# Three kept pieces instead of two in a down projection, with a new order table, in a two-layer attention encoder

## The chip, the cores and the metric

The kernel runs on one core of a Trainium2 chip. The metric is the device time of one execution in microseconds. A core has five instruction queues that run side by side: PE (matrix products and transposes), ACT (functions and copies), DVE (elementwise work), POOL (elementwise work and some transfers) and SP (transfers). Results of PE land in eight banks of 128 x 512 fp32 numbers, from which ACT and DVE read.

## The reference

Two layers over 512 tokens of width 1024, in fp32. Layer 0 mixes tokens with neighbourhood attention on a grid of 8 x 64, layer 1 with three groups of dilated attention. Each mixer ends in an output projection, and each layer in a SwiGLU block of inner width 2816:

```python
def swiglu(x, w_gate, w_up, w_down):
    return (jax.nn.silu(x @ w_gate) * (x @ w_up)) @ w_down
...
    for layer in range(DEPTH):
        h = rms_norm(x, norm_mix_pre[layer])
...
            h = neighbourhood_attention(h, na_w_qkv[j], na_w_o[j], na_rpb[j])
...
            h = dilated_attention(h, dil_w_qkv[j], dil_w_o[j])
        x = x + rms_norm(h, norm_mix_post[layer])
        h = rms_norm(x, norm_ffn_pre[layer])
        x = x + rms_norm(swiglu(h, ffn_w_gate[layer], ffn_w_up[layer], ffn_w_down[layer]), norm_ffn_post[layer])
```

## The kernel before

**Products.** Every fp32 operand is split into a high part h (ACT's copy, L415) and a low part l (DVE's subtraction, L416), and each fp32 product is three products of such parts (`mm3`, L426 to L430, so that one product shows as L427, L428 and L429). L427 and L429 read the high part of the moving operand, L428 its low part. Over blocks of the matrices runs a scheme with seven products in place of eight (`Seven`); its sums of weights are made on POOL and DVE (L495 to L501).

**Stages.** The time runs through: layer 0's projections and attention (to about 210 us), its output projection (tile names yo), gate and up projection (gu), down projection (yd); then the same for layer 1, whose attention runs from 590 to 1105 us. Tokens come in four tiles of 128. Between the output projection and the gate and up projection each tile is normed and transposed on PE (tr_o0_t_i: layer 0, tile t, part i; L649). A transpose's bank is emptied by ACT (L651, high part) and DVE (L652, low part); there are two such banks. L686 and L687 square and scale a half of a finished row of tiles, L633 and L635 (POOL) make its reciprocal root, L693 adds it to x.

**Down projection** (`down`, L937 to L1063). The inner width is cut into six pieces, five of two slots and one of one. For each piece the activations and the weights are split (`operands2`; the split weights take one of four slots), then multiplied into two banks, one for each of two tiles of tokens (`prod`, with ms the tiles done). The last two of the seven products both add into `left`, of which `left[0]` is tile 2 and `left[1]` tile 3. There the last pieces are kept and done for one tile, then for the other:

```python
                if i > last - 2:
                    kept.append(ops)
                else:
                    prod(left, ops)
...
        for m in range(2):
            for ops in kept:
                prod(left, ops, False, (m,))
```

**Order.** The order in which each queue runs its instructions isn't that of the code. `Order` collects all instructions with what they depend on, and `run` walks through them with costs of its own (`_cost`), taking on each engine the ready instruction of lowest rank. On PE it stays with the kind of the last matmul (plain, transposes, fp32) unless another is due by more than `stay`. `pin` (L317) repeats this forwards and backwards `times` times, takes the ranks of pass `FIRST`, and then goes through `TABLE`. A row of the table is (what, engine, lo, hi, turn, by): instructions of that engine (5: all) whose planned start (what 0 or 1) or whose number (what 2) lies from lo to hi get their rank moved by `by`, with what 0 from the rank they had in pass `turn`. One more walk gives the order, and each queue is tied to it.

Of the kernel before, what the change touches and what calls it, by code (L numbers as in the profile page):

```python
# [77 lines left out]
def _cost(i, e):  # L78
# [52 lines left out]

FIRST, TABLE = 11, (
# [28 lines left out]
)  # L163


class Order:
# [87 lines left out]
            for m in before:  # L254
                self.succ[m].append(n)

    stay = 1000.0

    def run(self, rank, back):

# [80 lines left out]
def encoder_kernel(ctx: ExitStack, tc: tile.TileContext, a: dict, out: bass.AP):  # L341
# [595 lines left out]
    def down(layer, hm, hl_, yp, more, sink):  # L937
# [3 lines left out]
        last = len(pieces) - 1  # L941
# [12 lines left out]
        def loaded(w):  # L954
            for i in range(last + 1):
                v = next(raw_)[:, :wp(w, i).shape[1]]
                nc.sync.dma_start(v, wp(w, i))
                yield v
# [75 lines left out]
        for n in range(2):  # L1034

            kept = []
            for i, w in enumerate(loaded(uab if n == 0 else every)):
                ops = operands2(xp((x1a, x2b)[n], i), w, f"{nm}{('s3', 'x2b')[n]}_{i}")
                if i > last - 2:
                    kept.append(ops)  # L1040
                else:
                    prod(left, ops)
                for f, *t in steps.get((n, i), ()):
                    f(*t)
            if n == 0:
# [3 lines that stand above are left out]
                    act.activation(y2u[m], left[m], AF.Copy)  # L1049
                for m in range(2):  # L1050
                    dve.tensor_sub(y2u[m], p5[m], y2u[m])
# [364 lines left out]
    order = [3 * j + g for j in range(PAIRS) for g in orders[j]]  # L1416
# [80 lines left out]
              for n, lo, hi, o, c, side in arenas]  # L1497
    order = Order(tc.nc.cur_bb.bb.instructions)
    order.link(tags, places, extra)
    order.pin(tc, 20, FIRST, TABLE)  # L1500


def _blocks(w, cols):
# [79 lines left out]
```

## Time and profile before

| | us |
|---|---|
| median of 3 runs | 1450.02 |
| lowest and highest run | 1445.73 and 1452.67 |
| the profiled execution | 1446.53 |
| its span, first to last instruction | 1444.7 |
| granted clock of PE, mean share of full speed | 0.997 |

The profile gives for each engine its busy time; for groups of instructions their line, their tile (out<-in) and form, busy time and mean; for a wait who waited and what ended it; and on a timeline each instruction with its start, its length and, in brackets, how long the engine stood idle before it and for whom. [...]

### The profile page before, as it was taken

How to read it: one execution, taken by the hardware profiler on the slowest of the kernel's cores; microseconds unless marked ns; L12 is line 12 of the kernel's file. 1: busy time of each engine (PE TensorE's matmuls, PEld its weight loads, DVE VectorE, ACT ScalarE, POOL GpSimd, SP SyncE). 2: the span in 40 equal slices, each digit the busy share in tenths (PEclk: the TensorE clock that was granted, in tenths of full speed). 3: DMA queues.
4: the chain of work that ended last, by engine and by line, in shares of the span. 5: the costliest groups of instructions: out<-in, count | busy, mean ns of one | idle time of the engine just before them, and what ended most of it. 6: DMA issues, size and time to landing. Idle time of an engine off the chain costs nothing. (4 is left out here: it accounts for less than half of the span.)

```text
span 1444.7 us, 27886 instructions
## 1 busy us (share of the span) xinstructions
PE 1412.8 (98%) x10764; PEld 1315.0 (91%) x10764; DVE 1182.1 (82%) x1882; ACT 905.0 (63%) x1822; POOL 557.4 (39%) x402
## 2 busy tenths in 40 slices
PE   7999999999999999999999999999999999999997
PEld 6988877999999888999989999999878999999886
DVE  6699967889998888888578777887657889998877
ACT  5478874555555657544477777887775555555664
POOL 5755525544330002766554434343215644340001
PEclk9999999999999999999999999999999999999999
DMA  6357587697234674445333343243766798844662
GB/s 235 112 181 193 168 298 211 217 268 205 89 117 147 196 229 158 162 159 183 125 103 111 111 146 120 82 139 104 253 185 245 200 246 236 261 142 154 209 213 95
DMA packets 86644, 253.20 MB, mean 175 GB/s; under 512 B 19312, under 2 KB 31600, under 8 KB 84464
## 3 DMA queue, kind: packets, MB, share of 16 engines
q1 hardware_dynamic: 77696, 197.69, 41.5%
q0 software_dynamic: 8672, 53.48, 14.4%
q8 instruction: 84, 1.38, 0.4%
q14 instruction: 48, 0.39, 0.1%
q10 hardware_dynamic: 144, 0.26, 0.0%
HBM read 229.24 MB, written 68.29 MB: 206 GB/s over the span
## 5 line engine op out<-in xcount | busy, mean ns | idle before, releaser
L635 POOL TENSOR_TENSOR rs_yd<-v_yd,mhalf 128x1 f32<-128x1 f32 x8 | 13.5, 1686 | 254.1 <-DVE v_yd L633 254.1
L427 PE MATMUL gu<-rxc,h_a 128*128 128x256 f32 x352 | 98.9, 283 | 1.4 <-ACT h_a L415 1.1
L428 PE MATMUL gu<-rxc,h_a 128*128 128x256 f32 x352 | 98.8, 281 | 1.3 <-DVE rxc L652 1.3
L429 PE MATMUL gu<-rxc,l_a 128*128 128x256 f32 x352 | 98.9, 282 | 0.0
L427 PE MATMUL gu<-rxa,h_c 128*128 128x256 f32 x352 | 98.5, 280 | 0.1
L429 PE MATMUL gu<-rxa,l_b 128*128 128x256 f32 x352 | 97.8, 278 | 0.2 <-DVE l_b L416 0.2
L428 PE MATMUL gu<-rxa,h_b 128*128 128x256 f32 x352 | 97.9, 278 | 0.2 <-DVE rxa L652 0.2
L428 PE MATMUL gu<-rxa,h_c 128*128 128x256 f32 x352 | 97.8, 278 | 0.0
L427 PE MATMUL gu<-rxa,h_b 128*128 128x256 f32 x352 | 97.8, 278 | 0.0
L429 PE MATMUL gu<-rxa,l_c 128*128 128x256 f32 x352 | 97.4, 278 | 0.0
L415 ACT ACTIVATE rxc<-mem 128x512 fp32r<-128x512 f32 (+2 forms) x92 | 57.6, 632 | 63.5 <-PE yd_pp L428 29.4
L495 POOL TENSOR_TENSOR r_d<-r_d 128x512 f32<-128x512 f32 x24 | 37.7, 1572 | 152.0 <-DVE l_ad L416 120.6
L416 DVE TENSOR_TENSOR rxc<-mem,rxc 128x512 fp32r<-128x512 f32 (+2 forms) x92 | 70.7, 776 | 20.6 <-ACT rxc L415 17.4
L495 POOL TENSOR_TENSOR r_gu<-r_gu 128x512 f32<-128x512 f32 x20 | 31.6, 1580 | 126.7 <-DVE l_a L416 69.8
L495 POOL TENSOR_TENSOR raw<-raw 128x512 f32<-128x512 f32 x24 | 40.3, 1682 | 91.6 <-DVE l_a L416 70.3
L427 PEld LDWEIGHTS gu<-rxc,h_a 128*128 128x128 f32 x352 | 67.0, 191 | 2.1 <-ACT h_a L415 1.3
L1297 ACT ACTIVATE mem<-mem 128x256 f32<-128x256 f32 x128 | 63.9, 503 | 7.7 <-DVE mem L1296 7.4
L428 PEld LDWEIGHTS gu<-rxc,h_a 128*128 128x128 f32 x352 | 67.3, 191 | 1.5 <-DVE rxc L652 1.5
L429 PEld LDWEIGHTS gu<-rxc,l_a 128*128 128x128 f32 x352 | 67.2, 191 | 0.0
L427 PEld LDWEIGHTS gu<-rxa,h_c 128*128 128x128 f32 x352 | 66.2, 188 | 0.7 <-DVE mem L893 0.3
L428 PEld LDWEIGHTS gu<-rxa,h_b 128*128 128x128 f32 x352 | 66.2, 188 | 0.6 <-DVE rxa L652 0.6
L429 PEld LDWEIGHTS gu<-rxa,l_b 128*128 128x128 f32 x352 | 66.2, 188 | 0.4 <-DVE l_b L416 0.4
(665 smaller groups left out, 6109.4 us busy)
## 6 DMA issues: line engine op xcount, KB each, us to landing
wsum<-wd POOLq DMA_DIRECT2D x24, 1408.0 KB, 11.7
r_d<-dil_qk SPq DMA_DIRECT2D x48, 512.0 KB, 4.2
raw<-wg SPq DMA_DIRECT2D x24, 512.0 KB, 4.9
raw<-wu SPq DMA_DIRECT2D x24, 512.0 KB, 7.5
wsum<-wsum POOLq DMA_DIRECT2D x8, 1408.0 KB, 9.7
raw<-wsum SPq DMA_DIRECT2D x22, 512.0 KB, 4.1
r_gu<-wg SPq DMA_DIRECT2D x20, 512.0 KB, 4.4
r_gu<-wu SPq DMA_DIRECT2D x20, 512.0 KB, 6.1
```

The lines of the kernel that those rows point to most:

```text
L415: act.activation(h, src, AF.Copy)
L416: dve.tensor_sub(l, src, h.bitcast(F32))
L427: i = pe.matmul(o, s[0], m[0], start=start, stop=False, skip_group_check=True)
L428: pe.matmul(o, s[0], m[1], start=False, stop=False, skip_group_check=True)
L429: pe.matmul(o, s[1], m[0], start=False, stop=stop, skip_group_check=True)
L495: self.added = e[0].tensor_add(q[0], q[0], q[2])
L635: pool.tensor_tensor(r, v, mhalf, op=ALU.pow)
L1297: act.activation(pr[:, f], pr[:, f], AF.Exp, bias=st[:, c:c + 1], scale=-1.0, accum_out=st[:, c + 2:c + 3])
```

## The change

The last three pieces are kept in place of two, in the last two products of the down projection of both layers. `stay` is 500 in place of 1000. The planner makes 12 passes in place of 20, and the table is another one: it starts from pass 1 in place of 11, and its 82 rows share none with the 83 of the old one.

```diff
-FIRST, TABLE = 11, (
-    (2, 0, 1975, 2245, 0, -1223), (1, 0, 1147819, 1157014, 0, -82769), (0, 5, 867142, 884029, 18, -5379),
...
+FIRST, TABLE = 1, (
+    (0, 5, 615418, 707297, 2, 55169), (1, 0, 1118715, 1130141, 0, -4617), (1, 2, 1129021, 1132931, 0, -8272),
...
-    stay = 1000.0
+    stay = 500.0
...
-                if i > last - 2:
+                if i > last - 3:
...
-    order.pin(tc, 20, FIRST, TABLE)
+    order.pin(tc, 12, FIRST, TABLE)
```

**The end of the kernel, PE.** yd1_s0 is the bank of tile 2, yd1_s1 that of tile 3, x2b_i the last product's piece i. Before, with nine rows of yd1_s1 from the fourth row here to the end:

```order
L427 MATMUL yd1_s0_15081<-h_d1x2b_5_15886,rxc_78 128x512
L428 MATMUL yd1_s0_15081<-l_d1x2b_5_15887,rxc_78 128x512
L429 MATMUL yd1_s0_15081<-h_d1x2b_5_15886,rxc_78 128x512
L427 MATMUL yd1_s1_15082<-h_d1x2b_4_15879,rxc_78 128x512
L428 MATMUL yd1_s1_15082<-l_d1x2b_4_15880,rxc_78 128x512
```

Of the change, with fifteen rows of yd1_s1 from the fourth row here to the end:

```order
L427 MATMUL yd1_s0_15081<-h_d1x2b_5_15874,rxc_78 128x512
L428 MATMUL yd1_s0_15081<-l_d1x2b_5_15875,rxc_78 128x512
L429 MATMUL yd1_s0_15081<-h_d1x2b_5_15874,rxc_78 128x512
L427 MATMUL yd1_s1_15082<-h_d1x2b_3_15859,rxc_78 128x512
L428 MATMUL yd1_s1_15082<-l_d1x2b_3_15860,rxc_78 128x512
```

Piece 3 has moved into the kept ones, and tile 2's last row stands six rows sooner. DVE's rows behind it are the same in both: L687 and L633 of tile 2, L687 and L633 of tile 3, L693 of tile 2, L693 of tile 3.

**Layer 0, from the output projection to the gate and up projection, PE.** yo0_3_h is half h of tile 3's output projection, gu0_f the product of feature tile f. Before:

```order
L428 MATMUL yo0_3_0_2692<-rxb0_92,rxa_77 128x512
L429 MATMUL yo0_3_0_2692<-rxb0_92,rxa_77 128x512
L427 MATMUL yo0_3_1_2693<-rxb0_92,rxa_77 128x512
L428 MATMUL yo0_3_1_2693<-rxb0_92,rxa_77 128x512
L429 MATMUL yo0_3_1_2693<-rxb0_92,rxa_77 128x512
L649 MATMUL tr_o0_0_0_2601<-ident_69,mem_79 128x128 x4
L649 MATMUL tr_o0_0_1_2608<-ident_69,mem_79 128x128 x4
L649 MATMUL tr_o0_1_0_2615<-ident_69,mem_79 128x128 x4
L649 MATMUL tr_o0_1_1_2622<-ident_69,mem_79 128x128 x4
L427 MATMUL gu0_0_2846<-rxc_78,h_a0_0_2847 128x256
L427 MATMUL gu0_1_2881<-rxc_78,h_a0_1_2882 128x256
L427 MATMUL gu0_2_2915<-rxc_78,h_a0_2_2916 128x256
```

Of the change:

```order
L649 MATMUL tr_o0_0_0_2601<-ident_69,mem_79 128x128 x4
L428 MATMUL yo0_3_0_2692<-rxb0_92,rxa_77 128x512
L429 MATMUL yo0_3_0_2692<-rxb0_92,rxa_77 128x512
L427 MATMUL yo0_3_1_2693<-rxb0_92,rxa_77 128x512
L428 MATMUL yo0_3_1_2693<-rxb0_92,rxa_77 128x512
L429 MATMUL yo0_3_1_2693<-rxb0_92,rxa_77 128x512
L649 MATMUL tr_o0_0_1_2608<-ident_69,mem_79 128x128 x4
L649 MATMUL tr_o0_1_0_2615<-ident_69,mem_79 128x128 x4
L427 MATMUL gu0_0_2846<-rxc_78,h_a0_0_2847 128x256
L427 MATMUL gu0_1_2881<-rxc_78,h_a0_1_2882 128x256
L649 MATMUL tr_o0_1_1_2622<-ident_69,mem_79 128x128 x4
L428 MATMUL gu0_0_2846<-rxc_78,h_a0_0_2847 128x256
```

The first four transposes moved ahead of the last five yo matmuls, the last four behind two gu matmuls, and gu0_2 back by some fifty rows. DVE at the same place, the change:

```order
L652 TENSOR_TENSOR rxc_78<-tr_o0_0_0_2601,rxc_78 128x4x128
L687 TENSOR_TENSOR mem_79<-yo0_3_0_2692,mem_79 128x512
L633 TENSOR_SCALAR few_small_80<-few_small_80 128x1
L687 TENSOR_TENSOR mem_79<-yo0_3_1_2693,mem_79 128x512
L652 TENSOR_TENSOR rxc_78<-tr_o0_0_1_2608,rxc_78 128x4x128
L652 TENSOR_TENSOR rxc_78<-tr_o0_1_0_2615,rxc_78 128x4x128
L693 SCALAR_TENSOR_TENSOR mem_79<-mem_79,few_small_80 128x1024
L652 TENSOR_TENSOR rxc_78<-tr_o0_1_1_2622,rxc_78 128x4x128
```

Before, both L687 and L633 stood first, and L693 stood ahead of both L652 of tile 1; now one L652 is ahead of L687, and one of tile 1's ahead of L693.

**Layer 1, the same place, PE.** Before:

```order
L649 MATMUL tr_o1_0_0_12277<-ident_69,mem_79 128x128 x4
L649 MATMUL tr_o1_0_1_12284<-ident_69,mem_79 128x128 x4
L428 MATMUL yo1_3_0_12371<-rxb1_6275,rxa_77 128x512
L429 MATMUL yo1_3_0_12371<-rxb1_6275,rxa_77 128x512
L427 MATMUL yo1_3_1_12372<-rxb1_6275,rxa_77 128x512
L428 MATMUL yo1_3_1_12372<-rxb1_6275,rxa_77 128x512
L429 MATMUL yo1_3_1_12372<-rxb1_6275,rxa_77 128x512
L649 MATMUL tr_o1_1_0_12291<-ident_69,mem_79 128x128 x4
L649 MATMUL tr_o1_1_1_12298<-ident_69,mem_79 128x128 x4
L427 MATMUL gu1_0_12528<-rxc_78,h_a1_0_12529 128x256
L427 MATMUL gu1_1_12563<-rxc_78,h_a1_1_12564 128x256
L428 MATMUL gu1_0_12528<-rxc_78,h_a1_0_12529 128x256
```

Of the change:

```order
L429 MATMUL yo1_3_1_12372<-rxb1_6275,rxa_77 128x512
L649 MATMUL tr_o1_0_0_12277<-ident_69,mem_79 128x128 x4
L649 MATMUL tr_o1_0_1_12284<-ident_69,mem_79 128x128 x4
L649 MATMUL tr_o1_1_0_12291<-ident_69,mem_79 128x128 x4
L649 MATMUL tr_o1_1_1_12298<-ident_69,mem_79 128x128 x4
L427 MATMUL gu1_0_12528<-rxc_78,h_a1_0_12529 128x256
L427 MATMUL gu1_1_12563<-rxc_78,h_a1_1_12564 128x256
L427 MATMUL gu1_2_12597<-rxc_78,h_a1_2_12598 128x256
L428 MATMUL gu1_0_12528<-rxc_78,h_a1_0_12529 128x256
```

Here the first eight transposes moved behind the last yo matmul, and gu1_2 moved up to be the third gu matmul. On DVE, L693 of the output projection stood behind all four L652 before and stands ahead of both L652 of tile 1 now; on ACT both L686 stood behind the first two L651 and stand ahead of them now.

54 rows, old and new, of the table c are left out of this document.

## The prediction

> **What bounds the kernel now.** I read the engines' busy time first, then the same table by stage, then PE's waits, and last the stretches where PE stands still.
>
> ```profile
> PE 1412.8 (98%) x10764; PEld 1315.0 (91%) x10764; DVE 1182.1 (82%) x1882; ACT 905.0 (63%) x1822; POOL 557.4 (39%) x402
> ```
>
> PE is busy for 1412.8 of 1444.7 us, so 31.9 us is all that any new order could take out of its idle time. The change leaves the arithmetic alone: PE's matmuls are as many before as after. The table by stage (start and end, length, then each engine's busy time and count, the granted clock, the DMA share, GB/s) says where the idle time lies:
>
> ```profile
> 75.00:210.00 135.00, 132.56 (x991) 114.48 (x991) 120.07 (x305) 111.46 (x275) 65.91 (x75) 1.00 0.65 198
> 252.00:575.00 323.00, 322.75 (x2337) 304.09 (x2337) 286.75 (x374) 188.93 (x315) 92.94 (x57) 0.99 0.57 180
> 590.00:1105.00 515.00, 510.70 (x4269) 480.12 (x4269) 390.36 (x715) 346.50 (x804) 226.65 (x146) 1.00 0.45 144
> 1113.00:1400.00 287.00, 286.60 (x2178) 273.83 (x2177) 255.51 (x333) 163.69 (x273) 88.77 (x59) 1.00 0.71 211
> ```
>
> Both feed-forward stages (252 to 575, 1113 to 1400) leave PE idle for 0.25 and 0.40 us. There is nothing to win there. The two attention stages hold 2.4 and 4.3 us, together 6.7. PE's longest waits (what waited, for what; us in total, times, longest):
>
> ```profile
> PE tr_a L649 <- DVE mem L642: 7.9, 1, 7.9
> ...
> PE pp_d L427 <- DVE mem L738: 1.0, 3, 0.4
> PE pp_n L427 <- DVE pp_n L485: 1.0, 1, 1.0
> ```
>
> The 7.9 us at the start stay, since PE's first 82 rows are the same in both orders. What remains are waits of about 1 us and the places between stages.
>
> **The kept pieces.** In the last product of a layer's down projection the kept pieces are done for tile 2, then for tile 3. With three kept, the second block grows from 9 to 15 matmuls, so tile 2's sum is complete six matmuls sooner. One takes 0.22 to 0.23 us (the last two start at 1435.95 and 1436.17), so 1.35 us sooner. The end of the kernel:
>
> ```profile
> 1435.95 0.39 PE L428 MATMUL yd_s<-l_d1x2b,rxc 128*128 128x512 f32 x1
> 1436.17 0.39 PE L429 MATMUL yd_s<-h_d1x2b,rxc 128*128 128x512 f32 x1
> ...
> 1438.28 1.45 POOL L635 TENSOR_TENSOR rs_yd<-v_yd,mhalf 128x1 f32<-128x1 f32 x1 [1.49 <-DVE v_yd L633]
> ...
> 1439.77 1.42 DVE L693 SCALAR_TENSOR_TENSOR mem<-memc,rs_yd,mem 128x512 f32<-128x512 f32 x2 [0.44 <-POOL rs_yd L635]
> ```
>
> The output's last part waits for tile 3: last matmul, square, POOL's reciprocal root (1.45 us from 1438.28), then L693 at 1439.77. PE's last matmul belongs to tile 3 in both orders, and DVE had already idled 0.44 us before that L693. Tile 2 coming sooner shortens nothing: **0**. What hides it is tile 3's own chain; if that were gone, at most 1.35 us could show. At layer 0 the sooner tile 2 meets a DVE queue that still has tile 3's split ahead: also 0, ends -1.4 and 0. Three kept pieces hold three of four weight slots. The next product has one slot at once, and the next when the first kept piece has been read, while 9 matmuls of the second block (2.0 us) and 12 of the next piece (2.7 us) are still to run. A split there is ACT's copy plus DVE's subtraction, 1.06 us and about as much again, so 2.4 us of cover remain: 0, and +1 if the cover goes.
>
> **Layer 0, output projection to feed-forward (246 to 252).** PE's timeline (start, length, idle time before in brackets):
>
> ```profile
> 246.03 1.04 PE L649 MATMUL tr_o<-ident,mem 128*128 128x128 f32 x8
> 248.48 1.26 PE L649 MATMUL tr_o<-ident,mem 128*128 128x128 f32 x8 [1.41 <-DVE rxc L652]
> 249.82 0.50 PE L427 MATMUL gu<-rxc,h_a 128*128 128x256 f32 x2
> 251.40 0.58 PE L427 MATMUL gu<-rxc,h_a 128*128 128x256 f32 x1 [1.08 <-ACT h_a L415]
> 251.78 0.42 PE L428 MATMUL gu<-rxc,h_a 128*128 128x256 f32 x1
> 252.00 0.42 PE L429 MATMUL gu<-rxc,l_a 128*128 128x256 f32 x1
> ```
>
> ACT's squares and the copies that empty the transposes' banks, on ACT and then DVE:
>
> ```profile
> 246.29 0.60 ACT L686 ACTIVATE mem<-yo 128x512 f32<-128x512 f32 x1
> ...
> 246.88 1.08 ACT L651 ACTIVATE rxc<-tr_o 128x512 fp32r<-128x512 f32 x2
> ```
>
> ```profile
> 246.33 0.69 DVE L687 TENSOR_TENSOR mem<-yo,mem 128x512 f32<-128x512 f32 x1 [2.12 <-ACT mem L686]
> ...
> 247.74 1.28 DVE L652 TENSOR_TENSOR rxc<-tr_o,rxc 128x512 fp32r<-128x512 f32 x2
> 248.94 1.28 DVE L693 SCALAR_TENSOR_TENSOR mem<-mem,few_small 128x1024 f32<-128x1024 f32 x1
> ```
>
> Before, all 16 transposes stand behind the last yo matmul. With two banks, the second eight wait for L652, which waits behind both L687. After, tr_o0_0_0 stands five yo matmuls sooner, at about 246.03 - 5 x 0.225 = 244.90. Its copy (half of 1.08) and subtraction (half of 1.28) then fall into DVE's idle 2.12 us; its bank is free by about 246.8, and the 1.41 us wait goes. The yo matmuls end 0.5 us later, so the second L687 does too, and L652 for tr_o0_1_0, now ahead of L693, ends near 249.8 (249.5 by that shift alone, up to 0.5 more for the copy that now stands ahead of the squares). The first L428 starts there and not at 251.78. What is late next is L652 of tr_o0_1_1, behind L693: 249.8 + 1.28 + 0.64 less overlaps = 251.6, by when PE has done 14 gu matmuls, against 3 in the order of before. That is 11 x 0.113 and the 0.1 between the two times: **-1.4** (ends -2.3, without that stall, and 0).
>
> The same place holds a second loss, which the clock column shows:
>
> ```profile
> 250.00:250.50 0.50, 0.32 (x2) 0.12 (x2) 0.50 (x2) 0.50 (x2) 0.50 (x1) 0.72 1.00 401
> 257.00:257.50 0.50, 0.50 (x6) 0.50 (x6) 0.46 (x1) 0.36 (x1) 0.50 (x1) 0.95 0.97 401
> ```
>
> The granted clock (the third number from the end) falls to a half at about 250.3 (0.72 over the half microsecond) and returns at about 257.05 (0.95), 6.8 us later; matmuls start every 0.22 us (251.78, 252.00) in place of 0.113 (the quick pace further below). From 251.78 to 257.05 that is 24 matmuls, each late by 0.107: **2.6 us**. In the 3.4 us up to the fall (half of 6.8) PE worked for about 1.1 us (the second eight transposes and two gu matmuls), 33%. At the end of the kernel it falls again:
>
> ```profile
> 1441.00:1442.00 1.00, 0.00 (x0) 0.00 (x0) 0.18 (x1) 0.00 (x0) 0.00 (x0) 0.73 0.95 361
> ```
>
> That is at 1441.5, not 3.4 us sooner, when PE had worked 1.9 us of 3.4 (from 1434.7 to the end of its last matmul; 56%). So the point lies between 33 and 56%. After the change the thinnest 3.4 us hold about 1.6 us of work (eight transposes and six gu matmuls; 47%): nearer to 56, so I take the clock as kept, **-2.6** (other end: the fall comes anyway, under denser work, +0.9).
>
> [...]
>
> **Layer 1, the same place (1106 to 1113).** Here the order goes the other way.
>
> ```profile
> 1108.18 1.25 PE L649 MATMUL tr_o<-ident,mem 128*128 128x128 f32 x8
> 1109.67 0.50 PE L427 MATMUL gu<-rxc,h_a 128*128 128x256 f32 x2 [0.24 <-ACT rxc L651]
> 1111.48 0.39 PE L428 MATMUL gu<-rxc,h_a 128*128 128x256 f32 x1 [1.31 <-DVE rxc L652]
> ```
>
> ```profile
> 1111.99 1.06 ACT L415 ACTIVATE h_a<-raw 128x1024 fp32r<-128x1024 f32 x1 [1.88 <-DMA raw<-wg]
> ```
>
> The rows are PE's, then ACT's. Before, eight transposes stood ahead of the last five yo matmuls. After, all 16 stand behind, so yo ends at 1107.4 and the squares of tile 3 precede every copy on ACT. Two squares (0.60 us each as at layer 0, and a sum read after each) run from about 1106.9, the copies from 1108.4; L652 for the first two banks, with an L687 between, ends near 1108.4 + 0.54 + 0.64 + 0.69 + 0.64 = 1110.9; L693 (1.28) now stands ahead of the L652 that PE needs, which ends near 1112.9. The third gu row also needs h_a1_2, whose data come by a transfer that starts after yo: 1111.95 - 0.8 + 1.06 = 1112.2, hidden by L652. First L428 at 1113.0 instead of 1111.48, with one more row done: **+1.4** (ends +0.5, if POOL and DVE are 0.9 sooner, and +2.1). From 1108.3 to 1113.0 PE works for about 1.2 us (eight transposes, three gu matmuls); no 3.4 us inside hold more than 36%, near the 33 that brought the fall. I take the fall; the half clock then covers 5.5 to 6.8 us of dense work: **+2.9** (ends 0 and +3.4).
>
> **Kind switches.** A 64-partition transpose or a plain fp32 matmul between the others costs PE a pause on either side:
>
> ```profile
> 121.87 0.28 PE L428 MATMUL pp_n<-rxb,h_bn 128*128 128x256 f32 x1
> 122.07 0.27 PE L812 MATMUL tb<-ident,mem 64*128 64x64 f32 x1
> 122.27 0.38 PE L429 MATMUL pp_n<-rxb,l_bn 128*128 128x256 f32 x1
> ```
>
> Starts are 0.20 apart instead of 0.113: 0.09 each. Counted over all of PE's rows, such switches rise from 169 to 187: 18 x 0.09 = **+1.6** (ends 0 and +2).
>
> **Attention stages.** Nearly every row moves. The producers of the two waits quoted last (2.0 us together) come sooner, those of others later. The same planner left 6.7 us of waits there before; I take as many after: **0**, with half of them, 3.4, as the bound to either side. In the feed-forward stages PE has no wait to lose, DVE is 89% busy, and new waits are possible: 0, ends 0 and +2.
>
> **Sum** against the profiled execution: -1.4 - 2.6 + 1.4 + 2.9 + 1.6 = +1.9, so 1446.53 + 1.9 = 1448.4. The profiled execution stood 3.5 us under the median of the runs, 1450.02, and I add the same 1.9 there: **1451.9**. A measurement of this kernel can tell about 0.5%, 7.2 us, from no change.
>
> **Rivals.** *Pace.* Matmuls of 128x256 run in two paces:
>
> ```profile
> 304.00:364.00 60.00, 60.00 (x528) 60.00 (x527) 8.96 (x24) 9.42 (x25) 1.00 0.80 231
> 370.00:408.00 38.00, 38.00 (x324) 38.00 (x323) 5.60 (x15) 5.91 (x16) 1.00 0.32 108
> ```
>
> That is 0.1136 and 0.1173 us each, both without waits and at full clock; the trace doesn't show what sets it. The four stages in the table above hold 991 + 2337 + 4269 + 2178 = 9775 matmuls; I estimate that two thirds, some 6,500, are of this shape. Half of them turned slow cost 3250 x 0.0037 = 12.0 us. *Slower*: the new order goes to and fro between output banks more often (1393 times, 1330 before); if that upsets the quick pace, two thirds of the 12.0, +8, give 1460. It decides once 22% of the 6,500 turn slow (1430 x 0.0037 = 5.3 us, which with the +1.9 make 7.2). Against it: the quick stretch from 304 to 364 has many bank changes too. *Faster*: half of the attention waits go without new ones (-3.4), layer 1 keeps its clock (-2.9), and a fifth of the matmuls turn quick (-4.8): 1451.9 - 11.1 = 1440.8. For it: the two waits whose producers come sooner; against it: three independent gains. [...] *No effect of the kept pieces* is already in the sum.
>
> **Numbers.** Forecast 0.38, clock kept 0.22, slower by pace 0.20, faster 0.20. The first two are within 0.5%: 0.60. The range takes in both outer cases and the bounds of the attention stages: 1440 to 1461; the likeliest case's own is 1447 to 1457.
>
> **What would show it.** Right: no clock fall near 250, one near 1112, DVE's L652 ahead of L693 at the first place and behind it at the second, the end unchanged from the last matmul on, 24 to 33 us of idle PE in all. Wrong: a wait of over 2 us inside an attention stage, a product's matmuls at another pace in most stretches, or a PE wait in the down projection on a weight slot.

## The result and the profile after

The changed kernel takes 1456.13 us (median of 8 runs, 1454.52 to 1459.77), the kernel before 1448.0 us beside it (8 runs, 1445.29 to 1452.67). The ratio is 1.006, with a 95% interval from 1.0045 to 1.0075: slower by 8.1 us. The profiled execution took 1454.52 us with a span of 1452.7, against 1446.53 and 1444.7. The engines' busy time:

```profile
PE 1415.5 (97%) x10764; PEld 1311.8 (90%) x10764; DVE 1193.2 (82%) x1882; ACT 903.3 (62%) x1822; POOL 554.8 (38%) x402
```

PE now stands idle for 1452.7 - 1415.5 = 37.2 us, 5.3 more than before, and its busy time has grown by 2.7 with as many matmuls: they start further apart in places. The table by stage, with the columns of before:

```profile
75.00:210.00 135.00, 130.97 (x975) 112.53 (x974) 121.24 (x304) 108.94 (x270) 66.59 (x74) 1.00 0.60 182
252.00:575.00 323.00, 320.61 (x2341) 301.00 (x2339) 287.93 (x380) 191.77 (x322) 92.31 (x62) 1.00 0.59 184
590.00:1105.00 515.00, 510.11 (x4275) 478.61 (x4274) 394.97 (x710) 344.67 (x804) 235.30 (x146) 1.00 0.46 143
1113.00:1400.00 287.00, 283.07 (x2163) 270.29 (x2164) 256.60 (x333) 162.28 (x271) 89.82 (x62) 0.99 0.71 209
```

The windows are fixed, so the work has slid a little under them. Still, the first attention stage idles for 4.0 us in place of 2.4, the second row for 2.4 in place of 0.25, and the last row, which begins at layer 1's place between the stages, for 3.9 in place of 0.4 and at a granted clock below 1. PE's longest waits now (what waited, for what; total, times, longest):

```profile
PE tr_a L649 <- DVE mem L642: 8.3, 2, 7.9
PE t L1393 <- ACT mem L1383: 2.3, 1, 2.3
PE pp_n L427 <- ACT h_an L415: 2.0, 2, 1.6
...
PE s L783 <- DVE mn L795: 1.0, 1, 1.0
```

All but the first are new or longer: one in layer 1's attention (at 1078), two in layer 0's. Where the 8 us come in shows best when the same row is looked up on PE's timeline of both kernels:

| start on PE, us | before | after | difference |
|---|---|---|---|
| first yo of layer 0 (mixer done) | 175.0 | 179.6 | +4.6 |
| first tr_n (layer 0 done) | 577.5 | 580.0 | +2.5 |
| sixth-last yo of layer 1 | 1105.9 | 1110.0 | +4.1 |
| last yd_s (PE done) | 1436.2 | 1444.1 | +8.0 |

So 4.6 us are lost in layer 0's mixer, 2.1 won from there to the end of layer 0, 1.6 lost in layer 1's mixer and 3.9 behind it. (The sixth-last yo has layer 1's first transposes behind it in both orders. The last yo, at 1108.0 and 1111.1, is not the same point of the work: eight transposes, 0.9 us, stand ahead of it before and behind it in the change.)

**Layer 0's mixer.** DVE, PE and ACT there (start, length, idle time before in brackets):

```profile
94.73 2.32 DVE L416 TENSOR_TENSOR l_cn<-r_n,h_cn 128x1024 fp32r<-128x1024 f32 x1
97.08 0.42 DVE L795 CUSTOM_DVE_ANT_0 mem<-s,mem 128x256 f32<-128x256 f32 x1
...
105.31 1.22 DVE L416 TENSOR_TENSOR l_bn<-r_n,h_bn 128x1024 fp32r<-128x1024 f32 x1
```

```profile
97.66 0.36 PE L783 MATMUL s<-rxc 128*128 128x256 f32 x1 [0.98 <-DVE mn L795]
...
105.20 0.38 PE L427 MATMUL pp_n<-rxa,h_an 128*128 128x256 f32 x1 [1.58 <-ACT h_an L415]
```

```profile
102.75 1.06 ACT L415 ACTIVATE h_bn<-r_n 128x1024 fp32r<-128x1024 f32 x1
...
104.11 1.04 ACT L415 ACTIVATE h_an<-r_n 128x1024 fp32r<-128x1024 f32 x1
```

The product s waits for a bank that L795 must read first, and L795 stands behind the long subtraction l_cn. Some 7 us on, pp_n waits for h_an, which ACT starts only at 104.11. Before, ACT was no sooner, and PE asked later:

```profile
104.61 1.05 ACT L415 ACTIVATE h_an<-r_n 128x1024 fp32r<-128x1024 f32 x1
```

```profile
108.35 0.28 PE L427 MATMUL pp_n<-rxa,h_an 128*128 128x256 f32 x1
```

In PE's order that matmul was row 774, behind those with h_bn; in the change it is row 735, ahead of them. The product s too was row 706 and is row 692. So both waits come as much from PE's rows, which ask sooner, as from the producers, which don't come sooner.

**Layer 0, output projection to feed-forward.** PE's timeline:

```profile
250.25 0.60 PE L649 MATMUL tr_o<-ident,mem 128*128 128x128 f32 x4
...
251.85 1.07 PE L649 MATMUL tr_o<-ident,mem 128*128 128x128 f32 x8
253.82 0.50 PE L427 MATMUL gu<-rxc,h_a 128*128 128x256 f32 x2 [0.90 <-ACT rxc L651]
...
254.89 0.39 PE L428 MATMUL gu<-rxc,h_a 128*128 128x256 f32 x1
255.12 0.28 PE L429 MATMUL gu<-rxc,l_a 128*128 128x256 f32 x1
255.23 0.28 PE L427 MATMUL gu<-rxc,h_a 128*128 128x256 f32 x1
```

From the last yo (251.62) to the first L428 pass 3.3 us in place of 6.0 before (245.8 to 251.78), and the matmuls behind start 0.11 us apart: the clock stays at full speed (1.00 from 246 to 264 us).

**Layer 1, the same place.** PE's timeline, then the clock by stretches of 2 us (third number from the end):

```profile
1111.37 1.03 PE L649 MATMUL tr_o<-ident,mem 128*128 128x128 f32 x8
1113.59 0.65 PE L649 MATMUL tr_o<-ident,mem 128*128 128x128 f32 x4 [1.18 <-DVE rxc L652]
1114.78 1.02 PE L649 MATMUL tr_o<-ident,mem 128*128 128x128 f32 x4 [0.54 <-DVE rxc L652]
1115.45 1.49 PE L427 MATMUL gu<-rxc,h_a 128*128 128x256 f32 x3
1117.64 0.58 PE L428 MATMUL gu<-rxc,h_a 128*128 128x256 f32 x1 [0.71 <-DVE rxc L652]
```

```profile
1114.00:1116.00 2.00, 1.46 (x9) 1.15 (x7) 1.02 (x3) 1.35 (x2) 1.67 (x2) 0.73 0.99 391
1116.00:1118.00 2.00, 1.16 (x4) 0.65 (x3) 2.00 (x3) 1.72 (x3) 0.00 (x0) 0.50 1.03 422
1118.00:1120.00 2.00, 2.00 (x11) 2.00 (x11) 2.00 (x4) 1.16 (x3) 0.54 (x1) 0.50 0.92 315
1120.00:1122.00 2.00, 2.00 (x12) 2.00 (x12) 1.56 (x2) 0.00 (x0) 2.00 (x2) 0.56 0.91 328
```

All 16 transposes stand in one row with two banks, so PE waits for L652 three times. L693, now ahead of both L652 of tile 1, itself waited for POOL:

```profile
1115.70 1.28 DVE L693 SCALAR_TENSOR_TENSOR mem<-mem,few_small 128x1024 f32<-128x1024 f32 x1 [0.98 <-POOL few_small L635]
```

The clock goes to a half at about 1114.9 (0.73 over that stretch) and back at about 1121.8 (0.56).

**The end.** PE's last matmul and the last L693:

```profile
1444.15 0.39 PE L429 MATMUL yd_s<-h_d1x2b,rxc 128*128 128x512 f32 x1
...
1447.74 1.42 DVE L693 SCALAR_TENSOR_TENSOR mem<-memc,rs_yd,mem 128x512 f32<-128x512 f32 x2 [0.44 <-POOL rs_yd L635]
```

From the one to the end of the span are 8.5 us, as before, and the 0.44 us of idle time is the same.

### The profile page after: what moved, and what is told of

The parts are those of the page before. It is cut to its first block, busy times and chain, and to the rows that moved or that the text cites. A ratio compares the mean times of both kernels' runs of the same rounds, so it can differ in the third digit from the quotient of the medians.

```text
span 1452.7 us, 27884 instructions
## 1 busy us (share of the span) xinstructions
PE 1415.5 (97%) x10764; PEld 1311.8 (90%) x10764; DVE 1193.2 (82%) x1882; ACT 903.3 (62%) x1822; POOL 554.8 (38%) x402
## 4 chain that ended last, share of the span: by engine, by line
PE 81%; DVE 8%; ACT 4%; DMA 4%; issue 2%; POOL 1%; SPq 0%; POOLq 0%; DVEq 0%; ACTq 0%
PE gu L427 9%; PE gu L428 9%; PE gu L429 9%; PE pp_d L427 5%; PE pp_d L429 5%; PE pp_d L428 5%; PE yd_s L427 3%; PE yd_s L429 3%; PE yd_s L428 3%; PE vd L427 2%; PE vd L428 2%; PE vd L429 2%; PE yd_pp L427 2%; PE yd_pp L429 2%; PE yd_pp L428 2%; PE t L1393 2%
## 5 line engine op out<-in xcount | busy, mean ns | idle before, releaser
L428 PE MATMUL gu<-rxc,h_a 128*128 128x256 f32 x352 | 98.4, 281 | 0.7 <-DVE rxc L652 0.7
L428 PE MATMUL gu<-rxa,h_b 128*128 128x256 f32 x352 | 97.4, 277 | 0.6 <-DVE rxa L652 0.6
L428 PE MATMUL gu<-rxa,h_c 128*128 128x256 f32 x352 | 97.4, 277 | 0.0
L428 PEld LDWEIGHTS gu<-rxc,h_a 128*128 128x128 f32 x352 | 67.0, 191 | 1.2 <-DVE rxc L652 1.2
L428 PEld LDWEIGHTS gu<-rxa,h_b 128*128 128x128 f32 x352 | 66.1, 188 | 0.8 <-DVE rxa L652 0.8
```

What stands on the lines that cost most here:

```text
L428: pe.matmul(o, s[0], m[1], start=False, stop=False, skip_group_check=True)
```

## The experiments

All kernels here have the program of the kernel before with the order of each queue written out, so that single rows or stretches can be moved. Those named a_ start from the change's order, with its fifteen rows of tile 3 at the end, those named b_ from the order of before. The change's order written out with nothing moved was not run; the nearest to it is a_wd below. The edit is of this kind:

```diff
-FIRST, TABLE = 1, (
+ORDER = (
...
-    order.pin(tc, 12, FIRST, TABLE)
+    order.fix(tc, ORDER)
```

The diffs below show rows of the queues. The kernel before was timed beside each group; ratios are against it.

### One stretch of the change put back into the order of before

**a_att0**: layer 0's mixer, on all queues. On POOL for instance, against the change:

```diff
 L496 TENSOR_TENSOR r_n_1179<-r_n_1179 128x512
-L927 DMA wsum_87<-wd 128x2816
 L497 TENSOR_TENSOR r_n_1179<-r_n_1179 128x512
...
 L501 TENSOR_TENSOR r_n_1179<-r_n_1179 128x512
+L927 DMA wsum_87<-wd 128x2816
```

> The changed kernel, with its order written out, and in it the instructions of layer 0's mixer up to its output projection (the first 2127 of the program) in the order of before, in the places that they hold in the changed order. Theory: in the changed kernel PE reaches the output projection 4.6 us later than before (179.6 against 175.0 us) because of new waits in this stage (1.14 at 97.7, 1.75 at 105.2 and smaller ones), so undoing it takes about 4.2 off: 4 us over before, ratio 1.0027. Rival: the stage is held up by DVE (89% busy) whatever the order, and the waits come back elsewhere in it: 7 to 8 us over before, ratio 1.005 or more. Rival pace: matmuls without waits are slower in the changed kernel; then the time stays at 8 over, with no wait left to show for it.

Measured: 1452.54 us, ratio 1.0036 (1.0023 to 1.005). The first yo stands 0.5 us later than before in place of 4.6, the end of PE 5.5 in place of 8.0. The ratio lies between the theory's 1.0027 and the rival's 1.005, and its interval overlaps the change's by a little. The mixer is some 2.5 to 3.5 us of the change's 8.1.

**a_b1**: layer 1 from the last stretch of its mixer to the start of gate and up. On PE:

```diff
+L649 MATMUL tr_o1_0_0_12277<-ident_69,mem_79 128x128 x4
+L649 MATMUL tr_o1_0_1_12284<-ident_69,mem_79 128x128 x4
 L428 MATMUL yo1_3_0_12371<-rxb1_6275,rxa_77 128x512
...
 L429 MATMUL yo1_3_1_12372<-rxb1_6275,rxa_77 128x512
-L649 MATMUL tr_o1_0_0_12277<-ident_69,mem_79 128x128 x4
-L649 MATMUL tr_o1_0_1_12284<-ident_69,mem_79 128x128 x4
 L649 MATMUL tr_o1_1_0_12291<-ident_69,mem_79 128x128 x4
```

> The changed kernel, with its order written out, and in it layer 1's output projection and the start of its gate and up projection in the order of before. Theory: this place costs 4.9 us in the changed kernel, 2.4 by waits and 2.5 by the clock that is halved from about 1115 to 1121 us; both go: 3.2 us over before, ratio 1.0022, and no half clock there (or a short one). Rival: the half clock is drawn by how windows fall, comes as often with the old order, and only the waits go: 5.7 us over before, ratio 1.004.

Measured: 1451.42 us, ratio 1.0029 (1.0016 to 1.0041), between the two expectations. The clock fell at this place here too, though for 3.4 us (1116.0 to 1119.5) and not 6.8: the short fall that the theory allowed, and in part what the rival said (what it calls windows shows in the traces as stretches of 3.41 us, told in the last section). The stretch includes the 2.3 us wait at 1078, which goes with it. In this profile the mixer of layer 0, which has the change's order, lost 6.5 us and not 4.6, because the clock fell there too (last section).

**a_both**: both stretches put back; all else, the kept pieces and layer 0's place included, as in the change.

> The changed kernel, with its order written out, and in it both places in the order of before: layer 0's mixer, and layer 1's output projection with the start of its gate and up projection. Theory: these two places are the whole loss (each undone alone took off about 3 to 4 of 8 us): 0 to 1.5 us over before, ratio 1.000 to 1.001. Rival: something else, spread over the stages (pace, switches, other waits), costs 3 us or more: ratio 1.002 or above.

Measured: 1446.58 us (12 runs), ratio 1.000 (0.999 to 1.001). The two stretches are the whole loss. What is left of the change, its kept pieces with them, is worth nothing that can be measured, to either side. In its profile the clock fell at layer 1's place for 3.4 us (1111.1 to 1114.5).

**a_b0**: layer 0, the output projection and the start of gate and up put back.

> The changed kernel, with its order written out, and in it layer 0's output projection and the start of its gate and up projection in the order of before. Theory: the new order gains about 1.4 by waits and 2.6 by the clock here, so with the old one the time is 8.1 + 4 = 12 us over before, ratio 1.0083, and the clock is halved for some 6.8 us near 255. Rival: the clock isn't a matter of this place's idle time, and stays: 9.5 us over before, ratio 1.0066.

Measured: 1467.02 us, ratio 1.0143 (1.0127 to 1.016): a miss for the theory and the rival. PE's waits of this kernel show where it lost:

```profile
PE gu L428 <- DVE rxa L652: 3.9, 4, 1.8
PE gu L427 <- ACT h_a L415: 3.7, 4, 2.3
```

These are in the gate and up projection behind the stretch; neither is above 0.7 us in the change. Presumably old rows ahead of new ones made waits of their own at the seam, so the time says nothing of the place itself. The clock did fall there for 6.8 us (256.0 to 262.9), as the theory said. Its counterpart follows.

### One part of the change put into the kernel before

**b_b0**: layer 0's place, by hand.

```diff
 L427 MATMUL yo_3_0_2692<-rxb_92,rxa 128x512
+L649 MATMUL tr_o_0_0_2601<-ident,mem 128x128 x4
 L428 MATMUL yo_3_0_2692<-rxb_92,rxa 128x512
...
-L649 MATMUL tr_o_0_0_2601<-ident,mem 128x128 x4
 L649 MATMUL tr_o_0_1_2608<-ident,mem 128x128 x4
...
+L652 TENSOR_TENSOR rxc<-tr_o_0_0_2601,rxc 128x4x128
 L687 TENSOR_TENSOR mem<-yo_3_0_2692,mem 128x512
...
-L693 SCALAR_TENSOR_TENSOR mem<-mem,few_small 128x1024
 L652 TENSOR_TENSOR rxc<-tr_o_1_0_2615,rxc 128x4x128
 L652 TENSOR_TENSOR rxc<-tr_o_1_1_2622,rxc 128x4x128
+L693 SCALAR_TENSOR_TENSOR mem<-mem,few_small 128x1024
```

> The kernel before, with its order written out, and by hand only the part of the change at layer 0's output projection that the prediction credits: the four transposes tr_o0_0_0 with their copies ahead of the last five yo matmuls, L693 behind the L652 of tile 1, the third gu matmul back at its product. Theory: the waits of 1.4 and 1.1 us go and the clock stays: 3.5 to 4.5 us under before, ratio 0.9973. Rival: the gain is taken back by later waits of this stage, as in the changed kernel (1.1 us at 267, 0.6 at 285): 2 us under before, ratio 0.9986. Rival: no gain.

Measured: 1446.25 us (12 runs), ratio 0.9998 (0.9988 to 1.0008). In its profile the clock stays up at 250, and PE is 2.9 us ahead at the end of layer 0 and 4.0 at the last yo of layer 1. At the end of PE 0.3 are left. The first part went at layer 1's place, where this kernel's clock falls and the kernel before's did not:

```profile
1107.00:1109.00 2.00, 1.47 (x7) 1.47 (x8) 1.66 (x2) 0.84 (x1) 0.12 (x1) 0.65 1.03 373
```

The rest went in the gate and up projection behind it: a new wait of 0.72 us for ACT's L507 at 1207, and a slower pace (from 1216 to 1266, without waits, 432 matmuls in place of 440), whose cause is open. The gain was not carried past this place.

**b_kept**: piece 3 of tile 3 moved into the kept ones, PE's rows alone, at four places like this:

```diff
-L427 MATMUL yd_s_5394<-h_d0s_3_6045,rxc 128x512
-L428 MATMUL yd_s_5394<-l_d0s_3_6046,rxc 128x512
...
 L429 MATMUL yd_s_5393<-h_d0s_5_6072,rxc 128x512
+L427 MATMUL yd_s_5394<-h_d0s_3_6045,rxc 128x512
+L428 MATMUL yd_s_5394<-l_d0s_3_6046,rxc 128x512
```

> The kernel before, with its order written out, and one thing changed: in the last two products of both down projections the six rows of piece 3 for the second tile stand behind the first tile's rows, as three kept pieces give. Theory: 0 within 1 us, since the last matmul is tile 3's in both and the chain behind it is tile 3's; the time from PE's last matmul to the end stays at 8.5 us. Rival: tile 2's sooner sum pays, 1.35 us at the end of each layer: 1.4 to 2.7 us under before. Rival: the third kept piece holds a slot too long: a PE wait on a weight split in the down projection, over 1 us above before.

Measured: 1449.52 us (11 runs), ratio 1.0012 (1.0003 to 1.0022), some 1.7 us by the ratio and 2.5 by the medians. PE's waits have a new row, in layer 0's down projection:

```profile
PE yd_s L427 <- ACT mem L1049: 0.8, 1, 0.8
```

L1049 is ACT's copy that empties the finished bank, so this isn't the wait on a weight split that the rival means, and 0.8 us aren't the whole loss. The chain behind the last matmul is unchanged. In the change this wait is below 0.1 us, presumably since ACT's and DVE's queues there are ordered for three kept pieces.

### The clock at layer 1's place

**a_fill1**: the change with 25 transposes of the identity in PE's waits there, 11 behind the first eight transposes, 5 behind the next four, 3 and 6 behind the second and third gu matmul. They go to a bank that gu overwrites.

```diff
-            self.i1 = prod(self.left, self.wa, 0, self.xs[X1A], True)
+            [Order.spare.add(pe.transpose(self.left[:, :P], ident, ident).ins.name) for _ in range(SPARE.get(self.name, 0))]; self.i1 = prod(self.left, self.wa, 0, self.xs[X1A], True)
...
+SPARE = {'1_3': 25}
```

> The changed kernel, with its order written out, and 25 more transposes of the identity matrix on PE, into a bank that nothing else uses yet, in the four waits at layer 1's output projection (11, 5, 3 and 6). They compute nothing that is used. Theory: the clock is halved there because PE is idle for most of a window; with the waits filled it stays at full, and the waits are as long as before: 2.5 us under the changed kernel, about 5.6 over before, ratio 1.0039. Rival: the clock falls for the transfers (400 GB/s at that time) or by chance: the fall is still there, 8.1 over before, ratio 1.0056. Rival: the extra transposes delay the real ones and cost 2 us or more: over 10.

Measured: 1451.99 us, ratio 1.0037 (1.0023 to 1.0052). The medians stand 5.2 us above the kernel before in place of 8.1; the two intervals still overlap by a little. The clock by stretches:

```profile
1114.00:1116.00 2.00, 2.00 (x17) 1.56 (x16) 1.61 (x3) 0.77 (x2) 2.00 (x3) 1.00 0.90 346
1116.00:1118.00 2.00, 1.60 (x14) 1.36 (x13) 1.41 (x2) 1.58 (x3) 0.56 (x2) 1.00 1.00 367
1118.00:1120.00 2.00, 1.80 (x16) 1.56 (x14) 2.00 (x3) 2.00 (x3) 0.00 (x0) 1.00 1.06 393
1120.00:1122.00 2.00, 2.00 (x20) 2.00 (x19) 1.56 (x4) 0.71 (x2) 1.65 (x2) 1.00 0.96 242
```

Same rows, same two banks, and no fall. From 1118 to 1122 PE starts 31 matmuls, one of them an extra transpose, where the change starts 20. The waits for L652 stay: from the last yo to the first L428 pass 6.5 us in both, 3.5 before.

**b_fill** and **b_best**: the same means in the kernel before, with 12 and 10 transposes at layer 0's place and 12 at layer 1's in b_fill, 12 and 12 in b_best. b_best was meant to have the part moved in b_b0 as well, and its expectation is for that. But the order written out in it is that of the kernel before on every queue: the first eight transposes stand at 245.94 us behind the last yo at 245.71. So the two together were not run.

```diff
+SPARE = {'0_3': 22, '1_3': 12}
...
+SPARE = {'0_3': 12, '1_3': 12}
```

> The kernel before, with its order written out, and more transposes of the identity matrix on PE, into a bank that nothing else uses yet, in the waits of layer 0's output projection (12 and 10) and of layer 1's (12). They compute nothing that is used. Theory: the clock no longer falls near 250 us, which saves 2.4 us in each execution in which it fell: 2 to 2.5 us under before, ratio 0.9984. Rival (the fall is not due to idleness): same as before.

> The kernel before, with its order written out, the part of the change at layer 0's output projection by hand (as in the run that moved only that), and 12 unused transposes of the identity matrix in the wait at each of the two output projections. Theory: that run was 4.0 us ahead of before until 1105 us, and lost it to a half clock at layer 1 (2 us) and a later wait; without the fall 2 to 3 us under before remain, ratio 0.998 to 0.9986. Rival: layer 1's gate and up stage is held by its transfers (DMA share 0.9 and more), and takes back whatever PE is early: 0 to 1 us under before.

Measured: 1445.5 us, ratio 0.9994 (0.9983 to 1.0004), and 1446.63 us, ratio 0.9993 (0.9982 to 1.0004). b_fill's interval holds both its theory's 0.9984 and no change at all. At both places the clock stays up, PE is 1.8 to 2.0 us ahead when layer 0 is done, and at the end of PE 0.7 ahead in b_best and 2.2 behind in b_fill: gate and up of layer 1 took it back, without a fall of the clock. No version was found that is clearly faster than the kernel before.

### The waits in layer 0's mixer

**a_han**: the change with ACT's h_bn and h_an ahead of three other rows.

```diff
+L415 ACTIVATE h_bn_1264<-r_n_1179 128x1024
+L415 ACTIVATE h_an_1414<-r_n_1397 128x1024
 L756 ACTIVATE rxc<-mem 64x512
 L757 ACTIVATE rxc<-mem 64x512
 L730 ACTIVATE mem<-pp_n_1182 128x256
-L415 ACTIVATE h_bn_1264<-r_n_1179 128x1024
 L1196 ACTIVATE mem<-mem,rc_1_912 128x256
-L415 ACTIVATE h_an_1414<-r_n_1397 128x1024
```

> The changed kernel, with its order written out, and in it on ACT the splits h_bn and h_an of layer 0's mixer moved ahead of the three instructions L756, L757 and L730 that stood before them (those wait for DVE while ACT idles 1.26 us). Theory: PE's wait of 1.75 us at 105 us is this queue order and nothing else; h_an is ready at 102.5 instead of 105.15, the wait goes, and PE reaches the output projection 1.3 to 1.7 us sooner than in the changed kernel, 178 us where the clock doesn't fall at 106: about 6.5 us over before in all. Rival: L756 and L757, now 2.1 us later, make PE wait for their own results, and nothing is gained or some is lost: 8 us over before or more.

Measured: 1461.85 us, ratio 1.010 (1.0086 to 1.0114). The wait stays, and what h_an waits for has changed:

```profile
104.25 1.06 ACT L415 ACTIVATE h_an<-r_n 128x1024 fp32r<-128x1024 f32 x1 [2.98 <-DMA r_n<-na_qk]
```

The theory that ACT's order alone holds h_an falls: ACT now stands before h_an until the transfer of r_n lands, and everything behind it is late: PE waits 2.84 us more at 108.7, and the clock falls.

**a_wd** and **a_wdcn**: these two are about the transfer. POOL issues a weight transfer at 95.92, just ahead of r_n's at 97.12; before, it stood at 103.04. a_wd moves that row back, a_wdcn also the subtraction l_cn.

```diff
-L927 DMA wsum_87<-wd 128x2816
 L497 TENSOR_TENSOR r_n_1179<-r_n_1179 128x512
...
 L1198 TENSOR_SCALAR mem<-mem,rc_1_912 128x256
+L927 DMA wsum_87<-wd 128x2816
...
-L416 TENSOR_TENSOR l_cn_1243<-r_n_961,h_cn_1242 128x1024
 L795 ISA mem,mn_1_910<-s_1_0_913,mem 128x256
 L795 ISA mn_1_910 128x1
+L416 TENSOR_TENSOR l_cn_1243<-r_n_961,h_cn_1242 128x1024
```

> The change with one row moved: POOL's weight transfer wsum<-wd of layer 0's mixer, issued at 95.92 us ahead of L497, stands behind L501 and two L1198 again, as in the kernel before (103.04 us there). Theory (the two halves of r_n, issued at 97.12, share the transfer engines with it and take about 7 us in place of 3 to 4, and h_an waits for them): r_n's data are there by about 101 us, h_an (L415) no longer stands idle for them, the 1.58 us wait of PE at 105 goes, first yo of layer 0 about 1.5 us sooner (+3.1 in place of +4.6 against the kernel before), and no clock fall at 106; ratio about 1.0045 to 1.005, against 1.006. Rival (the transfer is late for its late issue behind DVE's l_cn, whatever else is under way): the wait stays above 1 us and the ratio at 1.006.

> As a_wd, and DVE's 1024-wide subtraction l_cn (2.32 us at 94.73) stands behind the first L795 that PE's s waits for, not ahead of it. Theory (the 0.98 us wait at 97.66 is that subtraction on DVE's queue): it goes too, first yo of layer 0 about 2.5 us sooner than in the change (+2.1 against the kernel before), ratio about 1.004. Rival (a wait taken away there comes back one row later, because r_n is then issued still later and l_cn is itself what pp_n needs next): first yo no sooner than in a_wd, ratio as a_wd.

Measured: 1457.32 us, ratio 1.0048 (1.0034 to 1.0062), and 1455.02 us, ratio 1.0039 (1.0025 to 1.0053); neither can be told from the change's 1.006. The DMA issues from 94 to 110 us (KB each, median us from issue to landing), first of the change, then of a_wd:

```profile
r_n<-na_qk SPq DMA_DIRECT2D x2, 512.0 KB, 7.6
```

```profile
r_n<-na_qk SPq DMA_DIRECT2D x2, 512.0 KB, 4.1
```

The transfer does come 3.5 us sooner. But the wait stays at 1.62 us, because ACT runs h_an hardly sooner in its row (a_wd's timeline; 104.11 in the change):

```profile
103.57 1.04 ACT L415 ACTIVATE h_an<-r_n 128x1024 fp32r<-128x1024 f32 x1
```

So that wait has two holders that end within about half a microsecond of each other, the data and the place in ACT's queue, and with either one alone removed the other still holds it. Removing both at once was not tried, nor was putting PE's own row back behind those with h_bn. In a_wdcn the 0.98 us wait for L795 is gone, and the first yo stands 3.8 us later than before in place of 4.6: that one was the subtraction on DVE's queue. Its profiled execution, 1459.39 us, was its longest.

### The same rows in the main experiments

Starts on PE's timeline, as differences from the kernel before, in us:

| | change | a_att0 | a_b1 | a_both | a_fill1 | b_b0 | b_best |
|---|---|---|---|---|---|---|---|
| first yo of layer 0 | +4.6 | +0.5 | +6.5 | +0.9 | +5.9 | -0.1 | -0.1 |
| first tr_n | +2.5 | +0.6 | +4.6 | +0.4 | +4.6 | -2.9 | -1.8 |
| sixth-last yo of layer 1 | +4.1 | +1.1 | +3.3 | -0.8 | +5.0 | -4.0 | -2.5 |
| last yd_s | +8.0 | +5.5 | +5.5 | +0.2 | +7.2 | -0.3 | -0.7 |

## Why the prediction was right or wrong

The time lies inside the range and on the side of the sum, but the loss is four times the +1.9 of the sum. At 0.6% it has just left the case "within 0.5%", to which I gave 0.60. That it stands only 4.2 us above the forecast 1451.9 is in part luck: the 1450.02 that the forecast starts from, a median of three runs, is 2.0 us above that of the eight runs beside the change. Two of the forecast's own signs of being wrong came: 37.2 us of idle PE where 24 to 33 were named, and a wait of over 2 us inside an attention stage (2.3 us at 1078). The signs of being right came too for the clock, the order of L652 and L693 and the end. By stretches:

| stretch | forecast | profiles |
|---|---|---|
| layer 0's mixer | +1.6 | +4.6 |
| first yo of layer 0 to first tr_n | -4.0 | -2.1 |
| layer 1's mixer | 0 | +1.6 |
| sixth-last yo of layer 1 to PE's last matmul | +4.3 | +3.9 |
| behind it | 0 | 0 |

- **Attention stages, 0: the step that failed.** I reasoned that the same planner would leave as much waiting as before. In neither mixer did it. Layer 1's is 1.6 us longer, with the 2.3 us wait for ACT at 1078, which goes in a_b1 and a_both. In the first mixer, PE's waits from 84 to 180 us are, before and after:

```profile
PE s L783 <- POOL rxc L1182: 0.3, 1, 0.3
PE pp_n L427 <- DVE mem L738: 0.2, 1, 0.2
PE pp_n L427 <- ACT mem L507: 0.2, 1, 0.2
```

```profile
PE pp_n L427 <- ACT h_an L415: 2.0, 2, 1.6
PE s L783 <- DVE mn L795: 1.0, 1, 1.0
PE tb L809 <- POOL mem L1198: 0.3, 1, 0.3
PE pp_n L427 <- ACT mem L507: 0.2, 1, 0.2
```

  That is 3.5 in place of 0.7, +2.8: inside the bound of 3.4 that I gave, but on one side and not zero. The order of after was there to be read: l_cn directly ahead of the L795 that PE waits for, a weight transfer ahead of r_n's, and PE's own rows for s and h_an moved ahead. a_att0 and a_both show that the stretch is worth this much.
- **Kind switches, +1.6: right in size.** The forecast was for all of PE's rows, where they rise by 18. Nine of these lie in layer 0's mixer and eight in layer 1's. Measured between starts at the changes of kind, they cost about 1.2 us more in the first. With the waits that is 4.0 of the 5.3 us by which that mixer is longer (it starts 0.7 sooner); the rest is not traced.
- **Layer 0's place, -4.0: right in kind, too large.** The clock did not fall, and the first L428 came 2.7 us sooner behind the last yo. From the first yo to the first tr_n 2.1 are left; waits of 0.95 us at 267 (for L652, 0.15 before) and 0.41 at 285 (for a split) took back 1.2 of the difference, and the output projection, with four transposes now among its matmuls, takes 1.2 longer itself. Alone, in b_b0, the gain is 2.9 us at the end of layer 0 and nothing at the end of the kernel.
- **Layer 1's place, +4.3: right in mechanism, the sum nearer than its terms.** Three waits for L652, L693 ahead of two of them, and a fall of the clock from 1114.9 to 1121.8 where about 1112 was forecast for a kernel some 3 us ahead: +3.9. The waits cost 2.1 us up to the first L428 in place of the 1.4, since L693 itself waited 0.98 for POOL. The clock's part, 2.9 in the forecast, is what a_fill1 takes away: 2.9 us by the medians, whose intervals overlap, and some 1.6 in its profile (+2.3 in this stretch in place of +3.9). So one term was too small and the other probably too large, and that they make up for each other is luck. The case "clock kept" of the forecast's chances (0.22), no fall at either place, is refuted for this one. In the 3.4 us up to the fall PE worked for about 1.3 us (seven transposes, four, and one), 37% by the estimate of the last section, and never idled for more than 1.18 us at a time. That the share of work in the 3.4 us ahead decides was my estimate in the prediction, from one fall of 6.8 us, halved; falls of 3.4 us came in a_b1, a_both and a_fill1. The last section has what the traces show of the step and of where the point lies.
- **Kept pieces, 0: right for the change.** The end is the same to a tenth, and a_both has them at a ratio of 1.000. No PE wait on a weight slot appears. The 1.7 us of b_kept aren't the +1 "if the cover goes" of the forecast: its new wait is for the copy that empties a bank.
- **Pace: refuted.** The distances between starts of the quick matmuls hold 20.8 us over the quick pace before and 18.2 after, so the pace got no worse.

## What to carry to other kernels

When a whole order is replaced, compare the places where a queue's order changed next to a wait, in every stage, before calling a stage unchanged: here the loss lay in two stretches, one of which I had read closely and one of which I had set at zero. Look at both sides of such a place: a wait is also new where the waiting engine's own row moved ahead. A gain ahead of a stage that is bound otherwise must be followed to the end of the kernel; in b_b0 3 to 4 us were lost again 850 us later. And a wait with two holders that end together doesn't answer to removing one.

## What the runs showed of the hardware

**Where the clock can change, and from how little work.** In the profiles here the recorded changes of the clock lie whole multiples of 3.41 us apart (before: 250.22, 257.04 and 1441.47; the change: 1114.94, 1121.76 and 1449.44; a_fill1: 105.87, 109.29 and 1447.31), so each trace gives a grid of its own. The work in each stretch of that grid can be estimated from the starts of its matmuls, priced by their width at their usual distance at full clock (0.109 us for 128 columns, 0.114 for 256, 0.227 for 512). From the clock's first record on (14.7 us before, 15.8 in the change), the stretches with some work that a half clock followed hold 35 and 33% before (from 246.81 and 250.22), 37 and 30% in the change (from 1111.52 and 1114.94). The thinnest that full clock followed hold 51% before (from 1434.65), 45 and 46% in the change (from 101.17 and 1073.97). Between them lie two stretches of mixed work, a_wd's with 41% (101.95 to 105.36), followed by a half, and a_wdcn's with 39% (100.71 to 104.12), followed by full clock, which this estimate does not tell apart. So the point lies between 37 and 45%, and the 47% at which the prediction took the clock as kept was on the right side.

At layer 1's place the clock fell in six of six profiles with the change's rows and no extra transposes, in three of five with those of before (b_b0, a_b1, a_both; not in the kernel before and b_kept), and in none with extra transposes. At layer 0's place it fell in three of three profiles with the rows of before and no extra transposes, and in none of eight with those of the change (the change, a_att0, a_b1, a_both, a_fill1, a_han, a_wd and b_b0).

**The same rows, with and without a fall of the clock.** Five other kernels have PE's rows of the change at 103 to 107 us and its wait there, of 1.6 to 2.2 us (a_b1, a_b0, a_fill1, a_wd, a_wdcn); in the profiles of the first four the clock falls there, in a_wdcn's and the change's it doesn't. First the change, then a_fill1:

```profile
105.00:107.00 2.00, 1.80 (x13) 1.57 (x14) 2.00 (x7) 2.00 (x9) 0.00 (x0) 1.00 0.06 23
107.00:109.00 2.00, 2.00 (x19) 2.00 (x19) 1.72 (x4) 1.95 (x7) 0.27 (x1) 1.00 0.36 98
```

```profile
105.00:107.00 2.00, 2.00 (x12) 1.55 (x12) 1.63 (x5) 2.00 (x9) 0.00 (x0) 0.72 0.03 10
107.00:109.00 2.00, 2.00 (x10) 2.00 (x10) 1.87 (x4) 1.95 (x5) 0.29 (x1) 0.50 0.33 98
```

From about 105.9 to 109.3 a_fill1 runs at half speed, 3.4 us, which costs 1.3 us at the first yo (+5.9 against +4.6). In the four profiles with a fall the whole wait lies inside one stretch of the grid (a_fill1: 103.37 to 104.96, the stretch from 102.46 to 105.87). In the other two a line of the grid cuts the wait (the change: 103.61 to 105.20, the line at 104.59; a_wdcn: 102.82 to 104.41, the line at 104.12), and the clock stayed up. So with a gap of this size the clock fell in four of six profiles, and in these six it went with where the lines of the grid lay. The change's own runs have mean clocks of 0.998 to 0.994 and times of 1454.5 to 1459.8 us. That this spread comes from such falls was not tested.

**A long subtraction beside POOL.** DVE's 128x1024 subtraction takes 1.22 us at 105.31 and 2.32 us at 94.73 (both rows above). Beside the second one POOL had this row in the change:

```profile
94.69 1.28 POOL L496 TENSOR_TENSOR r_n<-r_n 128x512 f32<-128x512 f32 x1
```

The extra 1.1 us are about the length of that row. This was read from the trace and not tested.
